# The first mixer's two attentions written as one list of steps

## The chip, the core and the metric

The kernel runs on one core of a Trainium2 chip. A core has five engines with an instruction queue each: TensorE (PE, matrix products; its weight loads are shown apart as PEld), VectorE (DVE), ScalarE (ACT), GpSimd (POOL) and SyncE (SP, which here only issues DMAs). They work on a shared on-chip memory, and PE writes its sums to eight banks of 128 x 512 floats that DVE and ACT read. The metric is the device time of one execution in microseconds, lower is better.

## What is computed

A decoder trunk of two layers on 512 tokens of width 1024, all in float32. Layer 0 has a mixer of two attentions side by side, layer 1 another mixer; each layer ends in a gated ConvFFN. Only the first mixer matters here:

```python
def even_mixer(h, w_in, ...):
    c_q, c_kv, k_rope, dq, dk, dv = split_cols(h @ w_in, EVEN_SPLITS)
    q = heads_first(rms_norm(c_q, cq_g) @ w_uq, MLA_HEADS)        # 8 heads
    kv = heads_first(rms_norm(c_kv, ckv_g) @ w_ukv, MLA_HEADS)
    o_mla = mla_attention(q_nope, q_rope, k_nope, rope(k_rope, pos), v_mla)
    lam = (jnp.exp(jnp.sum(lam_q1 * lam_k1)) - jnp.exp(jnp.sum(lam_q2 * lam_k2)) + lam_init)
    o_diff = diff_attention(dq[:, :, 0], dq[:, :, 1], dk[:, :, 0], dk[:, :, 1], dv, lam, slopes)  # 4 heads
    o_diff = rms_norm(o_diff, subln_g) * (1.0 - lam_init)
    return jnp.concatenate([heads_last(o_mla), heads_last(o_diff)], axis=-1) @ w_out
```

Latent attention is a causal softmax over 8 heads. Differential attention has 4 heads; each takes two softmaxes with a distance bias, and the second, times `lam`, is subtracted from the first before the values are applied.

## The kernel before

The 512 tokens are four tiles of 128 (`NT`), taken in the order 3, 2, 1, 0 (`ORDER`). Products with weights are done in three passes that together keep float32 precision (`mm3`, lines 261 to 265): high part by high part, high by low, low by high. One `mm3` is called a triple here. A weight arrives as a raw tile by a DMA on SP and is split by `Weights.split`: ACT writes the high part (line 72), DVE subtracts it to get the low part (line 73). `Weights.next` hands out the next weight and first splits as many ahead as `depth` says; `load` only issues the DMA. Activations are split alike by `split` (lines 171 and 172).

The instructions are traced in the order of the program, but a planner then chooses the order on each engine from costs that it expects. Only inside `tc.manual_schedule(engines=...)` do the instructions of the engines named stay in the order written. Before the change the mixer has one such block, the output projection at its end.

The mixer (`even`, line 573) has these stages:

- Norm and transposes of x, the compressed projections, and the query/key projections of differential head 0 (lines 618 to 674), then the queries, keys and values of the latent heads (675 to 699).
- Latent attention (701 to 773). A unit is a head pair `p2`, a query tile `i` and a head of the pair `z`: 32 units. `score` (705) makes one score product (line 709), adds the mask and takes the row minimum on DVE (the table-add, line 593), takes the exponential and its sum on ACT (597), and on DVE the reciprocal (712) and the scale (713). `turn` (719) transposes the blocks on PE (727) and copies them out, on ACT for odd heads (737) and on DVE for even ones (739). `value` (742) multiplies by the values once per head pair (750) and splits the result into `oM` (752). `skewed` issues stage d of unit n - d in each round; the value projection of the differential heads, `diff_v` (757), is issued between and after, one tile of 24 matmuls at a time. The planner mixes all of this.
- Differential attention (776 to 905). A unit is a head and a tile: 16 units. `score` makes two score products in two banks (827), two table-adds, two exponentials, and combines them on DVE (838 to 841); `turn` transposes and copies (604 to 609); `value` multiplies (852), scales, squares on ACT (856) and takes the reciprocal root on POOL (178 to 181); `norm` scales again (863); `finish` transposes a whole head and splits it into `oD` (870, 871). Between every second pair of rounds there is a filler: a query/key projection `diff_qk`, and at the end the first half of the output projection's terms for tiles 3 and 2 (`early`). The tables (bias `alibi`, norm gain, `lam`) are loaded at the start of this stage (779 to 797).
- The output projection (910 to 931), a manual block: for each tile two halves of the columns and two halves of the terms (`project`), the residual with its norm, and the next norm's transposes, one tile behind.

Memory tiles come from pools; tiles of one tag share `bufs` buffers, and a tile waits until the one before it in its buffer has been read. Weights' halves have 5 buffers (`wpool`), raw tiles 3, and the eight banks are shared by tags: "a" 3, "s" 2, "t", "n" and "o" 1 each.

Of the kernel before, what the change touches and what calls it, by code (L numbers as in the profile page):

```python
# [9 lines left out]
F32 = mybir.dt.float32  # L10
# [7 lines left out]
P = 128  # L18
S = 512
# [67 lines left out]
def trunk(tc, A, out):  # L87
# [3 lines left out]
    with ExitStack() as top:  # L91
# [5 lines left out]
        GAP = 32  # L97
# [475 lines left out]
        def even():  # L573
            with ExitStack() as es:
# [12 lines left out]
                xh, xl = xnT  # L587

                def softmax_negated(sc, ps, table, n, bufs, reads=None):

                    s = sc.tile([P, S], F32, tag="s", name="s", bufs=bufs)
                    st = sc.tile([P, 2], F32, tag="st", name="st", bufs=6)
                    m = DVE.tensor_tensor_reduce(out=s[:, :n], in0=ps, in1=table, scale=1.0, scalar=3e38,
                                                 op0=ALU.add, op1=ALU.min, accum_out=st[:, 0:1])
                    if reads is not None:
                        reads.append(m.ins.name)
                    ACT.activation(s[:, :n], s[:, :n], AF.Exp, bias=st[:, 0:1], scale=-1.0,
                                   accum_out=st[:, 1:2])
                    return s, st

                def transposed(sc, s, nb, on_act, tag, bufs=3):
                    tp = bank(tag, "tpp", 4, P)
                    for j in range(nb):
                        PE.transpose(tp[:, j], s[:, j * P:(j + 1) * P], ident[:])
                    pt = sc.tile([P, 4, P], F32, tag="pt", name="pt", bufs=bufs)
                    if on_act:
                        ACT.copy(pt[:, :nb], tp[:, :nb])
                    else:
                        DVE.tensor_copy(pt[:, :nb], tp[:, :nb])
                    return pt  # L610


                with ExitStack() as e1:
# [8 lines left out]
                    def diff_qk(h, z):  # L622
                        acc = bank("a", "aqk")
                        wh, wl = W.next()
                        for k in range(KD):
                            mm3(acc, wh[:, k * P:(k + 1) * P], wl[:, k * P:(k + 1) * P],
                                xh[:, k], xl[:, k], k == 0, k == KD - 1)
                        if z == 0:
                            ACT.activation(dq[h], acc, AF.Copy, scale=-0.125)
                        else:  # L630
                            DVE.tensor_copy(dk[h], acc)

                    with ExitStack() as e2:
# [4 lines left out]
                        cT = (cp.tile([P, 3, S], F32R, tag="cth", name="cth"),  # L638
                              cp.tile([P, 3, S], F32R, tag="ctl", name="ctl"))
# [33 lines left out]
                        for z in range(2):  # L673
                            diff_qk(0, z)
# [27 lines left out]
                    mmask = sc.tile([P, S], F32, tag="mmask", name="mmask")  # L702
                    nc.scalar.dma_start(mmask[:], A["mla_mask"])

                    def score(p2, i, z):
                        def f(_):
                            h, w = 2 * p2 + z, (i + 1) * P
                            s_ps = bank("s", "sps")
                            PE.matmul(s_ps[:, :w], mq[h][:, i * P:(i + 1) * P], mk[h][:, :w], start=True, stop=True)
                            s, st = softmax_negated(sc, s_ps[:, :w], mmask[:, 384 - i * P:], w, 3)  # L710
                            rd = sc.tile([P, 1], F32, tag="rd", name="rd", bufs=4)
                            DVE.reciprocal(rd[:], st[:, 1:2])
                            DVE.tensor_scalar(s[:, :w], s[:, :w], rd[:, 0:1], None, ALU.mult)
                            return s
                        return f

                    pts = {}
                    off = (0, 512, 896, 1152, 1280)

                    def turn(p2, i, z):  # L720
                        def f(s):
                            if i == 0:
                                pts[p2, z] = sc.tile([P, 1280], F32, tag="pt", name="pt", bufs=3)
                            pt = pts[p2, z]
                            tp = bank("tn"[z], "tpp", 4, P)
                            for j in range(i + 1):
                                PE.transpose(tp[:, j], s[:, j * P:(j + 1) * P], ident[:])

                            for j in range(0, i + 1, 2):
                                n = min(2, i + 1 - j)  # L730
                                c = off[j] + (i - j) * P
                                d = off[j + 1] - off[j] - P
                                o = pt[:, c:c + P] if n == 1 else pt[:, c:c + 2 * d].rearrange(
                                    "p (a b) -> p a b", a=2)[:, :, 0:P]
                                t = tp[:, j] if n == 1 else tp[:, j:j + 2]
                                if z:
                                    ACT.copy(o, t)
                                else:
                                    DVE.tensor_copy(o, t)
                        return f  # L740

                    def value(p2, i, z):
                        def f(_):
                            if i < NT - 1 or z == 0:
                                return
                            o = bank("o", "o")
                            for j in range(NT):
                                for y in range(2):
                                    h = 2 * p2 + y
                                    PE.matmul(o[y * 64:(y + 1) * 64, j * P:], mv[:, j, h * 64:(h + 1) * 64],  # L750
                                              pts[p2, y][:, off[j]:off[j + 1]], start=(j == 0), stop=(j == NT - 1))
                            split(oM[0][:, p2], oM[1][:, p2], o)
                        return f

                    wv = []

                    def diff_v(i):
                        if not wv:
                            wv.extend(W.next() for _ in range(4))
                        t = slice(i * P, (i + 1) * P)  # L760
                        a = bank("a", "av")
                        for k in range(KD):
                            wh, wl = wv[k // 2]
                            c = slice((k % 2) * 512, (k % 2 + 1) * 512)
                            mm3(a, xh[:, k, t], xl[:, k, t], wh[:, c], wl[:, c], k == 0, k == KD - 1)
                        if i % 2 == 0:
                            DVE.tensor_copy(dv[:, i], a)
                        else:
                            ACT.copy(dv[:, i], a)

                    skewed([[g(p2, i, z) for g in (score, turn, value)]
                            for p2 in range(4) for i in range(NT) for z in range(2)],
                           [lambda i=i: diff_v(i) for i in range(NT)], 100)


                sc = es.enter_context(tc.tile_pool(name="esd", bufs=1, reuse_waits="tile"))
                oD = (sc.tile([P, 4, S], F32R, tag="odh", name="odh"),
                      sc.tile([P, 4, S], F32R, tag="odl", name="odl"))
                subg = sc.tile([P, P], F32, tag="subg", name="subg")
                nc.scalar.dma_start(subg[:], A["ev_subln_g"][0:1, :].partition_broadcast(P))  # L780
                lamb = sc.tile([P, 4, 64], F32, tag="lamb", name="lamb")
                nc.scalar.dma_start(lamb[:], A["ev_lam"].partition_broadcast(P))
                reads = []
                neglam = sc.tile([P, 1], F32, tag="neglam", name="neglam")
                alibi = sc.tile([P, 4, S], F32, tag="alibi", name="alibi")
                nc.scalar.dma_start(alibi[:], A["alibi"])
                lj = sc.tile([P, 64], F32, tag="lj", name="lj")
                ls = sc.tile([P, 2], F32, tag="ls", name="ls")
                for z in range(2):
                    DVE.tensor_tensor_reduce(out=lj[:], in0=lamb[:, 2 * z], in1=lamb[:, 2 * z + 1], scale=1.0,  # L790
                                             scalar=0.0, op0=ALU.mult, op1=ALU.add, accum_out=ls[:, z:z + 1])
# [53 lines left out]
                def turn(h, i):  # L845
                    return lambda s: transposed(sc, s, i + 1, i % 2, "t")
# [552 lines left out]
```

## Time and profile before

| | us |
|---|---|
| runs: median of 3 (lowest, highest) | 1167.63 (1166.95, 1168.72) |
| profiled execution, its span | 1165.2 |
| PE busy | 1145.4 |
| DVE busy | 812.3 |
| ACT busy | 556.9 |
| mean granted clock of PE | 0.998 |

The span of the profiled execution runs from its first to its last instruction. The profile's page has the whole, and the trace behind it answers by line, by stretch of time and by instruction. A row of a group names the line, engine and operation, what it writes and reads, the shapes and the count, then the busy time and the mean length in ns, then how long the engine stood idle just before these instructions and what ended that. In a row of the timeline the first two numbers are the start and the length in us; a bracket at the end has the idle time before it and its releaser.

### The profile page before, as it was taken

What the parts mean: (1) busy time and instruction counts of PE and PEld (TensorE: products, weight loads), DVE (VectorE), ACT (ScalarE), POOL (GpSimd) and SP (SyncE); (2) the same over time, 40 slices, a digit from 0 to 9 for tenths busy, and PEclk for the clock granted to TensorE, in tenths of its full rate; (3) what the DMA queues carried; (4) which work ended last, traced back from release to release, by engine and by line L of the source; (5) the groups of instructions that cost most, each with busy time, mean ns of one, the idle gap of its engine ahead of it and who ended that gap; (6) DMA issues with size and microseconds to landing.
All of it is one profiled execution on the core that took longest, in us unless ns stands there. A gap on an engine that the chain in (4) does not pass through costs nothing.

```text
span 1165.2 us, 15209 instructions
## 1 busy us (share of the span) xinstructions
PE 1145.4 (98%) x5668; PEld 939.9 (81%) x5668; DVE 812.3 (70%) x1431; ACT 556.9 (48%) x940; POOL 57.5 (5%) x137
## 2 busy tenths in 40 slices
PE   8999999999999999999999999999999999999997
PEld 8876667898888888888878877898988888888886
DVE  6677676457766767899873465666676766779896
ACT  5565555245444444456553454544444444445562
POOL 2100012110000000000020000002000000000002
PEclk9999999999999999999999999999999999999999
DMA  8320521033332332354735212322232323324461
GB/s 283 115 64 1 169 73 38 37 130 127 95 104 91 104 95 82 109 159 155 246 108 159 73 55 91 91 74 83 95 116 91 102 98 91 106 84 136 138 214 72
DMA packets 39049, 126.81 MB, mean 109 GB/s; under 512 B 4672, under 2 KB 6336, under 8 KB 38848
## 3 DMA queue, kind: packets, MB, share of 16 engines
q1 hardware_dynamic: 37056, 122.11, 32.8%
q10 hardware_dynamic: 1920, 3.74, 1.0%
q8 instruction: 44, 0.72, 0.3%
q14 instruction: 29, 0.24, 0.1%
HBM read 117.95 MB, written 6.29 MB: 107 GB/s over the span
## 4 chain that ended last, share of the span: by engine, by line
PE 45%; issue 2%; DVE 1%; POOL 1%; ACT 1%; POOLq 0%; DVEq 0%; ACTq 0%
PE u L265 7%; PE u L264 7%; PE u L263 7%; PE acc L263 3%; PE acc L265 3%; PE acc L264 3%; PE apt L263 3%; PE apt L264 3%; PE apt L265 2%; PE cp L1064 1%; PE apv L263 1%; PE apv L265 1%; PE apv L264 1%; PE o L1148 1%; PE o L1225 1%
## 5 line engine op out<-in xcount | busy, mean ns | idle before, releaser
L73 DVE TENSOR_TENSOR wl<-wraw,wh 128x1024 fp32r<-128x1024 f32 (+1 forms) x202 | 244.5, 1218 | 182.2 <-ACT wh L72 178.0
L72 ACT CAST wh<-wraw 128x1024 fp32r<-128x1024 f32 (+1 forms) x202 | 209.4, 1046 | 281.2 <-PE u L264 179.6
L264 PE MATMUL u<-xl,wh 128*128 128x512 f32 (+1 forms) x768 | 285.3, 372 | 0.1
L265 PE MATMUL u<-xh,wl 128*128 128x512 f32 (+1 forms) x768 | 285.2, 372 | 0.0
L263 PE MATMUL u<-xh,wh 128*128 128x512 f32 (+1 forms) x768 | 285.0, 372 | 0.1
L264 PEld LDWEIGHTS u<-xl,wh 128*128 128x128 f32 x768 | 144.7, 188 | 25.3 <-DVE xl L172 0.3
L263 PEld LDWEIGHTS u<-xh,wh 128*128 128x128 f32 x768 | 144.5, 188 | 25.4 <-ACT xh L171 0.6
L265 PEld LDWEIGHTS u<-xh,wl 128*128 128x128 f32 x768 | 144.7, 188 | 24.9
L264 PE MATMUL acc<-wl,gh 128*128 128x512 f32 (+1 forms) x250 | 96.9, 387 | 0.0
L265 PE MATMUL acc<-wh,gl 128*128 128x512 f32 (+1 forms) x250 | 96.9, 387 | 0.0
L263 PE MATMUL acc<-wh,gh 128*128 128x512 f32 (+1 forms) x250 | 96.8, 388 | 0.0
L417 ACT ACTIVATE y<-y 128x512 f32<-128x512 f32 x44 | 27.7, 632 | 85.1 <-DVE y L415 85.1
L412 ACT ACTIVATE y<-u,cw 128x512 f32<-128x512 f32 x88 | 67.4, 773 | 1.8 <-PE u L265 1.8
L415 DVE SCALAR_TENSOR_TENSOR y<-u,cw,y 128x510 f32<-128x510 f32 x88 | 65.6, 748 | 2.5
L413 DVE SCALAR_TENSOR_TENSOR y<-u,cw,y 128x511 f32<-128x511 f32 x88 | 65.1, 744 | 0.9 <-ACT y L412 0.9
L178 POOL TENSOR_TENSOR rv<-ms,epst 128x1 f32<-128x1 f32 x39 | 11.0, 285 | 924.1 <-ACT junk L230 843.9
L263 PEld LDWEIGHTS acc<-wh,gh 128*128 128x128 f32 x250 | 46.9, 188 | 10.0 <-issue 0.6
L265 PEld LDWEIGHTS acc<-wh,gl 128*128 128x128 f32 x250 | 46.9, 188 | 9.7
L264 PEld LDWEIGHTS acc<-wl,gh 128*128 128x128 f32 x250 | 46.9, 188 | 9.6
L263 PE MATMUL apt<-xh,wh 128*128 128x512 f32 x128 | 50.6, 395 | 0.0
L264 PE MATMUL apt<-xl,wh 128*128 128x512 f32 x128 | 50.0, 391 | 0.0
L265 PE MATMUL apt<-xh,wl 128*128 128x512 f32 x128 | 49.9, 390 | 0.0
(305 smaller groups left out, 1911.3 us busy)
## 6 DMA issues: line engine op xcount, KB each, us to landing
wraw<-in_ffn_w_up SPq DMA_DIRECT2D x88, 512.0 KB, 3.6
wraw<-in_ffn_w_down SPq DMA_DIRECT2D x44, 512.0 KB, 3.7
wraw<-in_od_w_dqk SPq DMA_DIRECT2D x12, 512.0 KB, 3.6
wraw<-in_ffn_w_down SPq DMA_DIRECT2D x22, 256.0 KB, 2.6
wraw<-in_ev_w_dqk SPq DMA_DIRECT2D x8, 512.0 KB, 4.0
wraw<-in_ev_w_out SPq DMA_DIRECT2D x8, 512.0 KB, 3.7
spill<-X SPq DMA_DIRECT2D x8, 512.0 KB, 2.6
X<-spill SPq DMA_DIRECT2D x8, 512.0 KB, 6.6
```

Of the source, the lines that this page charges most:

```text
L72: self.nc.scalar.copy(h[:, :w], raw[:, :w])
L73: self.nc.vector.tensor_tensor(l[:, :w], raw[:, :w], h[:, :w].bitcast(F32), ALU.subtract)
L263: PE.matmul(o, lh, rh, start=first, stop=False, skip_group_check=more)
L264: PE.matmul(o, lh, rl, start=False, stop=False, skip_group_check=more)
L265: PE.matmul(o, ll, rh, start=False, stop=last, skip_group_check=more)
L412: ACT.activation(y[:, z], u, AF.Identity, bias=c[:, 3:4], scale=c[:, 2:3])
L413: DVE.scalar_tensor_tensor(y[:, z, 1:], u[:, :S - 1], c[:, 1:2], y[:, z, 1:], ALU.mult, ALU.add)
L415: DVE.scalar_tensor_tensor(y[:, z, 2:], u[:, :S - 2], c[:, 0:1], y[:, z, 2:], ALU.mult, ALU.add)
L417: ACT.activation(y[:, 0], y[:, 0], AF.Silu)
L1064: PE.matmul(zp[:, c + (j2 - j) * P:c + n], tri[:, 0 if j2 == j else 1], part[:, off[j2]:off[j2 + 1]], start=(j2 == j and part is sh), stop ...
L1148: PE.matmul(o12[hp][:, y, r], pt[:, y, rr, g], cv12[:, r, c:c + 64], start=(g == 0), stop=(g == 1))
L1225: PE.matmul(o[:, h], pt[:, h, b * P:(b + 1) * P], cv[:, j0 + b, h * 64:(h + 1) * 64], start=(b == 0), stop=(b == nb - 1))
```

## The change

Latent and differential attention are written out as two loops, one after the other, in manual blocks that name PE, DVE, ACT and POOL. `skewed`, `transposed` and the nested stage functions go. The core of the first loop, with `M` = 32 units:

```diff
+ W.depth = 1
+ wv = [W.next() for _ in range(4)]
+ made = {2: 14, 21: 15, 25: 16, 29: 17}
+ fill = Fill(diff_v((3, 2)), diff_v((1, 0)), *[diff_qk(h, z) for h in range(1, 4) for z in range(2)])
+ with tc.manual_schedule(engines=everything):
+     for n in range(M + 2):
+         if n + 2 in made:
+             W.load()
+         m = n - M
+         if 0 <= n - 1 < M:
+             m_scale(n - 1)
+         if m == 1:
+             d_combine(0)
+         if 0 <= n - 2 < M:
+             m_turn(n - 2)
+         if n < M:
+             m_score(n)
+         else:
+             d_score(m)
+         if n % 8 == 2 and n > 8:
+             o = m_values(n // 8 - 1)
+         fill(1 if n < M else 3)
+         if n % 8 == 3 and n > 8:
+             split(oM[0][:, n // 8 - 1], oM[1][:, n // 8 - 1], o)
+         if n in made:
+             W.ahead(made[n])
+     o = m_values(3)
```

`m_score` is the score product, the table-add and the exponential; `m_scale` the reciprocal and the scale; `m_turn` and `m_values` are the old `turn` and the matmuls of `value`. `Fill` holds generators and issues one triple per count. `diff_v` now takes two tiles at a time, into two "a" banks, with the two tiles' triples of one weight block behind each other:

```diff
+ def diff_v(tiles):
+     accs = [bank("a", "av") for _ in tiles]
+     for k in range(KD):
+         wh, wl = wv[k // 2]
+         c = slice((k % 2) * 512, (k % 2 + 1) * 512)
+         for a, i in zip(accs, tiles):
+             if k or i != tiles[0]:
+                 yield
+             t = slice(i * P, (i + 1) * P)
+             mm3(a, xh[:, k, t], xl[:, k, t], wh[:, c], wl[:, c], k == 0, k == KD - 1)
```

The core of the second loop, with `N` = 16 units; `quota` gives the triples of each step, and `made` the ten steps that end in a weight split (each one's DMA is issued a step earlier):

```diff
+ early = [(i, half) for i in (3, 2, 1) for half in range(2)]
+ fill.parts += [project(*e, 0) for e in early]
+ made = {3: (W, 18), 5: (W, 19), 6: (W2, 1), 7: (W, 20), 8: (W2, 2), 9: (W, 21), 10: (W2, 3),
+         11: (W, 22), 13: (W, 23), 15: (W, 24)}
+ quota = [0, 0] + [5] * 2 + [4] * 8 + [3] * 4 + [4] * 3
+ with tc.manual_schedule(engines=everything):
+     W.ahead(17)
+     split(oM[0][:, 3], oM[1][:, 3], o)
+     for m in range(2, N + 3):
+         if m + 1 in made:
+             made[m + 1][0].load()
+         if 0 <= m - 3 < N:
+             d_norm(m - 3)
+         if m - 1 < N:
+             d_combine(m - 1)
+         if m - 2 < N:
+             d_turn(m - 2)
+         if m < N:
+             d_score(m)
+         n = quota[m]
+         fill(n - n // 2)
+         if m - 2 < N:
+             d_value(m - 2)
+         if (m - 3) % 4 == 3 and m > 3 and m < N + 2:
+             d_finish((m - 3) // 4)
+         fill(n // 2)
+         if m in made:
+             w, k = made[m]
+             w.ahead(k)
...
+     fill.end()
+     d_finish(3)
```

`d_score` is two score products, two table-adds and two exponentials; `d_combine` the four DVE operations that combine them; `d_turn`, `d_value`, `d_norm` and `d_finish` are the old stages (`d_finish` uses bank "n" for heads 0 to 2). The output projection's block follows in the same manual block; tile 1's first half of the terms is now among the early ones.

The rest: a function `tables`, called before the latent heads' queries are made, issues five DMAs on ACT's queue for the bias (in two buffers that the norm used), the mask (into `dv[:, 0]`, which the value projection overwrites only at its end), the norm gain and the lambda vectors, and computes `lam` there; the old loads of these go. The compressed vectors `cT` are now views of `oM`. Score tiles come from a pool `sx` with 4 buffers for both attentions (before 3 and 5). `new_xnT` is called later, `W.depth` is 5 again after the block, and some spacers that place buffers change size.

More of the change, by code (lines that the diff above doesn't have):

```diff
@@ L742, in value @@
[L742 to L769, printed above, removed]
@@ L782, in even @@
[L782 to L791, printed above, removed]
```

322 lines of the change are left out of this document (170 added, 152 removed).

## The prediction

> **What bounds the kernel now.** I read the page's totals first, then the busy time by stage, then the two attention stages in order of time.
>
> ```profile
> span 1165.2 us, 15209 instructions
> PE 1145.4 (98%) x5668; PEld 939.9 (81%) x5668; DVE 812.3 (70%) x1431; ACT 556.9 (48%) x940; POOL 57.5 (5%) x137
> ...
> 64.00:130.80 66.80, 66.70 (x317) 44.55 (x316) 46.65 (x173) 35.91 (x104) 0.00 (x0) 1.00 0.17 53
> 130.80:207.50 76.70, 72.74 (x381) 52.18 (x381) 54.97 (x183) 40.79 (x118) 13.88 (x32) 1.00 0.27 85
> 207.50:242.00 34.50, 34.50 (x163) 28.75 (x162) 15.74 (x21) 13.03 (x28) 5.09 (x16) 1.00 0.11 46
> ```
>
> A stage row reads: length, then busy time of PE, weight loads, DVE, ACT, POOL, then the granted clock. The stages are latent attention with the value projection (64.0 to 130.8), differential attention with the query/key projections (to 207.5), and the output projection (to 242.0, where the first ConvFFN's matmuls begin). PE looks full, but its ends are modelled, so I price its work from start to start.
>
> ```profile
> 65.01 0.39 PE L263 MATMUL av<-wh,xh 128*128 128x512 f32 x1
> 65.69 0.39 PE L263 MATMUL av<-wh,xh 128*128 128x512 f32 x1
> ...
> 84.91 1.88 PE L709 MATMUL sps<-mk,mq 128*128 128x512 f32 x4
> 86.62 0.49 PE L727 MATMUL tpp<-ident,s 128*128 128x128 f32 x3
> 86.95 0.39 PE L709 MATMUL sps<-mk,mq 128*128 128x128 f32 x2
> ...
> 117.46 2.42 PE L750 MATMUL o<-pt,mv 128*64 128x512 f32 x15
> ...
> 132.01 0.92 PE L827 MATMUL sps<-dqk 64*128 64x384 f32 x4 [0.78 <-DVE st L593]
> 140.05 1.16 PE L852 MATMUL o<-dv,pt 128*128 128x128 f32 x8
> ```
>
> Three projection matmuls (one "triple") take 0.68 (65.01 to 65.69). A 512-wide score takes 0.86 (two in 1.71), so 0.215 per block of 128; a transpose 0.11; a head pair's latent values 2.4. A differential score pair costs 0.215 per block too (0.92 less a tail of 0.28, over 3), differential values 0.22 per block. Work in 64.0 to 207.5: 80 latent score blocks 17.2, 80 transposes 8.8, 32 triples 21.8, values 9.6; then 64 triples 43.5, 40 score blocks 8.6, 40 transposes 4.4, 40 value blocks 8.8, 16 closing transposes 1.8. Together 124.5 of 143.5 us: PE loses about 19 us to waits. That is all that a better order can win.
>
> **What the change does, part by part.** It adds no arithmetic. It fixes the order on PE, DVE, ACT and POOL, moves tables and 8 triples of projection (tile 1, first half of the terms) forward, and pairs value tiles.
>
> Is a written list kept literally? The old kernel has one, in the output projection:
>
> ```profile
> 227.99 0.55 POOL L181 TENSOR_TENSOR rr<-rv,mhalf 128x1 f32<-128x1 f32 x1
> ...
> 231.27 0.69 DVE L225 TENSOR_TENSOR t<-ao,gain 128x512 f32<-128x512 f32 x1 [3.84 <-ACT junk L230]
> 231.88 1.40 DVE L876 SCALAR_TENSOR_TENSOR t<-X,rr,gain 128x512 f32<-128x512 f32 x2
> ```
>
> L876 had its scale at 228.54, and DVE idled 3.84, yet it ran after L225, as written. So I take the list as literal.
>
> *Latent list.* Step n puts on DVE: reciprocal and scale of unit n-1, copy of unit n-2 (even heads), table-add with minimum of unit n. The reciprocal of n is then next on DVE, and needs ACT's exponential of n. Nothing stands between, so DVE waits out each exponential, and PE's transposes two steps on wait for that scale.
>
> ```profile
> 67.61 0.28 DVE L593 CUSTOM_DVE_ANT_0 s<-sps,mmask 128x128 f32<-128x128 f32 x1
> ...
> 72.16 0.16 DVE L712 RECIPROCAL rd<-st 128x1 f32<-128x1 f32 x1
> 72.36 0.42 DVE L713 TENSOR_SCALAR s<-s,rd 128x384 f32<-128x384 f32 x1
> ...
> 73.63 0.69 DVE L593 CUSTOM_DVE_ANT_0 s<-sps,mmask 128x512 f32<-128x512 f32 x1
> 74.42 0.72 ACT L597 ACTIVATE s<-s,st 128x512 f32<-128x512 f32 x1
> 75.27 0.16 DVE L712 RECIPROCAL rd<-st 128x1 f32<-128x1 f32 x1
> 75.94 0.48 DVE L713 TENSOR_SCALAR s<-s,rd 128x512 f32<-128x512 f32 x1
> 76.34 0.28 DVE L593 CUSTOM_DVE_ANT_0 s<-sps,mmask 128x128 f32<-128x128 f32 x1
> ...
> L597 ACT ACTIVATE s<-s,st 128x128 f32<-128x128 f32 (+3 forms) x32 | 17.9, 563 | 9.3 <-DVE st L593 7.2 <-DVE rd L712 2.0
> L593 DVE CUSTOM_DVE_ANT_0 s<-sps,mmask 128x128 f32<-128x128 f32 (+3 forms) x32 | 15.3, 482 | 5.0 <-PE sps L709 4.0 <-PE tpp L727 1.0
> L713 DVE TENSOR_SCALAR s<-s,rd 128x128 f32<-128x128 f32 (+3 forms) x32 | 12.3, 383 | 0.6
> L739 DVE COPY pt<-tpp 128x256 f32<-128x256 f32 (+1 forms) x24 | 8.6, 371 | 2.1 <-PE tpp L727 2.0
> L73 DVE TENSOR_TENSOR wl<-wraw,wh 128x1024 fp32r<-128x1024 f32 x3 | 3.6, 1220 | 0.8 <-ACT wh L72 0.8
> L171 ACT CAST omh<-o 128x512 fp32r<-128x512 f32 x4 | 2.3, 586 | 7.2 <-PE o L750 7.2
> L72 ACT CAST wh<-wraw 128x1024 fp32r<-128x1024 f32 x2 | 2.1, 1052 | 0.0
> L172 DVE TENSOR_TENSOR oml<-o,omh 128x512 fp32r<-128x512 f32 x3 | 2.1, 685 | 0.0
> ```
>
> At 512 wide: table-add to exponential 0.79 (0.10 over its length), exponential to reciprocal 0.85 (0.13 over), reciprocal to scale 0.20, scale to the next table-add 0.40 (0.08 under). With the means over the four widths: 0.48 + 0.10 + 0.56 + 0.13 + 0.20 + 0.30 = 1.78 us a unit, 56.9 for 32. Copies: 24 x 0.29 = 7.0. Four weight splits and three output splits stand at the ends of steps, exactly there: ACT's half queues behind the exponential, DVE's half then stands ahead of the next reciprocal. A weight split adds 1.05 + 1.22 less 0.09 of overlap, 2.2, an output split 1.2: 8.8 + 3.6. Sum 76.3 on DVE, against 55.0 of PE work in the same steps (17.2 + 8.8 + 21.8 and three values at 2.4). The old order needed 66.8 for latent attention and the same value triples, as it put other units' DVE work under each exponential.
>
> The first table-add stood at 67.61, right behind a weight split; I keep that start (bounds 65 to 68), so the list's last scale ends at 67.6 + 76.3 = 143.9. Then the last transposes 0.44, a score 0.64, three triples 2.04 and the last values 2.4 bring PE to 149.4.
>
> *Differential list, 17 steps.* Ten steps end in a weight split.
>
> ```profile
> L840 DVE SCALAR_TENSOR_TENSOR s<-s,den 128x512 f32<-128x512 f32 (+3 forms) x16 | 8.8, 550 | 0.0
> L863 DVE SCALAR_TENSOR_TENSOR otok<-otok,rr,subg 128x128 f32<-128x128 f32 x16 | 5.6, 349 | 10.6 <-POOL rr L181 10.5
> L839 DVE SCALAR_TENSOR_TENSOR den<-den,st,neglam 128x1 f32<-128x1 f32 x16 | 3.5, 217 | 1.5 <-ACT s L597 1.3
> L609 DVE COPY pt<-tpp 128x384 f32<-128x384 f32 (+1 forms) x8 | 3.3, 417 | 0.0
> L856 ACT ACTIVATE jk<-otok 128x128 bf16<-128x128 f32 x16 | 4.9, 307 | 12.4 <-DVE otok L854 12.3
> ```
>
> There the loop runs: table-add 0.58 with its hop, two exponentials 1.12, square 0.31, cast 1.05, DVE's half 1.22, then norm 0.27, reciprocals 0.30, the factor 0.22, combine 0.47, and half the time a copy 0.34: 5.7 with mean widths; these ten steps are narrower (2.1 blocks against 2.5) and two of the pieces overlap their neighbours, so 5.35. Ten make 53.5; two head splits among them add 1.0, five evacuations of query/key sums 2.8: 57.3. The seven plain steps run at PE's pace (step 2: four transposes 0.44, a two-block score 0.43, four value blocks 0.88, five triples 3.4): 5.2 + 4.2 + 3.6 + 4.2 + 3.4 + 3.1 + 3.2 = 26.9. Where the two kinds meet, in five places, PE's value matmuls wait for a copy that stands behind the step before's split; I take 1 us each (bounds 0 and 2): 5. The list then ends at 149.4 + 57.3 + 26.9 + 5 = 238.6.
>
> *Output projection.* 34.5 less the 8 moved triples (5.4) is 29.1; the first transposes of the next norm come 0.7 too early for their rows (estimate from 0.69 + 1.40 of DVE after the last sum against 2.7 of PE). End: 268.4 instead of 242.0.
>
> *Costed at nothing.* The pairing keeps its 96 matmuls. The tables: the old mask's issue cost ACT 0.39; five such are 2 us, under an ACT that idles 2.57 twice in that stretch.
>
> ```profile
> 51.15 0.58 ACT L693 COPY mk<-auk 64x512 f32<-64x512 f32 x1 [2.57 <-PE auk L265]
> ...
> 64.07 0.39 ACTq L703 DMA_DIRECT2D mmask<-in_mla_mask  x1
> ```
>
> Without that cover it is 2 us. The old table loads at 120 lay under value triples, so nothing is won there. Loads on SP are issued one to three steps (over 5 us) ahead of their splits.
>
> The sum: +26.4 on 1165.2 is a span of 1191.6; the runs' median lies 2.4 above the span, so 1194.
>
> **The rivals.**
>
> *PE sets the pace after all, and the list removes its waits (faster).* Then the latent list is PE's 55.0, the two first differential steps and the last values 8.0, and the differential steps are 66 triples 44.9, 33 score blocks 7.1, transposes, values and closings 15.0: from 64.0 to 194.0, projection to 223.1, so -19: 1149. For it: the page's 98% on PE. Against: at w = 512 PE has 1.97 a unit, while DVE's and ACT's own chain is 2.24 before copies. It decides only if DVE work can slip under an exponential. The Trainium skill ("Perfetto Trace Analysis", section "Identifying the Most-Contended Engine") says to work on the engine with the highest occupancy; by that rule the filling of PE's gaps is the whole result, which is this rival.
>
> *Only the latent half loses.* The differential waits vanish into PE's work: 149.4 + 67.0 = 216.4, projection to 246.2: +4.2, 1172. For it: there, exponentials have half a step of PE work and the square before DVE needs them. Against: ten splits are queued in DVE's way.
>
> *The list isn't literal* and the planner's order mostly stays: 1168.
>
> A clock loss would top the forecast up. Twice (steps 6 and 10) a head's split and a weight's stand behind each other on DVE, and PE's value matmuls could then wait up to 0.69 + 1.22 + 0.27 + 0.30 + 0.22 + 0.47 + 0.34 = 3.5 us.
>
> ```profile
> 0.00:20.00 20.00, 16.15 (x81) 14.62 (x82) 10.07 (x15) 11.15 (x18) 4.04 (x16) 0.91 0.79 273
> ```
>
> Only where PE idled early was the clock 0.91; the stage rows above have 1.00, and I add nothing. The Trainium skill ("TensorE: Matmul & The Clock Gate", section "Part 1: The HAM clock gate (the "warmup" mystery)") has the clock halve after an idle window of about 3.4 us and stay so for another; by that rule two such waits would cost up to 3.4 us more.
>
> **How the numbers follow.** Forecast 0.74, only the latent half 0.12, PE's pace 0.09, list not literal 0.05. The forecast's own range is 1184 to 1206: 0.10 more or less per hop is 3 us, the seams 5, the start 3, an uncounted wait in each differential step some 5. Reaching down past the second rival gives 1169 to 1206, with about 0.2 outside (the first and third rival, and the forecast's top). A measurement tells 0.2% (2.3 us) from no change. Slower: 0.74 + 0.12 + 0.01 = 0.87; faster 0.09 + 0.02 = 0.11; same 0.02.
>
> **What would show it.** In the latent stage DVE idles before each reciprocal, released by the exponential, about 0.8 a unit, and PE's transposes wait for the scale; the last 32nd unit's scale lies near 144. In the differential stage DVE's half of a split waits 1 to 2.5 us for ACT, and PE's value matmuls wait for DVE's copy. The first ConvFFN matmul lies near 268. I am wrong if reciprocals follow without a wait, or if the first ConvFFN matmul lies before 242.

## The result, and the profile after

The changed kernel takes 1195.81 us (median of 4 runs, 1193.37 to 1197.56) against 1167.43 us for the kernel before on the same chip: a ratio of 1.0241, 95% interval 1.0226 to 1.0255. It is slower by 28.4 us; forecast were 1194 and a range of 1169 to 1206.

The page's head and the busy time by stage for the changed kernel. The first stage ends with the last latent values (in the kernel before, it ended with the rest of the value projection, which came behind them), the second with the start of the last head's closing transposes, the third with the first ConvFFN matmul.

```profile
span 1193.6 us, 15204 instructions
PE 1149.9 (96%) x5668; PEld 939.8 (79%) x5668; DVE 815.0 (68%) x1431; ACT 554.8 (46%) x940; POOL 55.4 (5%) x139
...
64.00:150.80 86.80, 71.52 (x330) 43.92 (x329) 50.19 (x175) 36.81 (x108) 0.46 (x2) 0.96 0.12 37
150.80:239.40 88.60, 77.10 (x388) 56.13 (x387) 53.22 (x173) 37.85 (x113) 11.82 (x32) 0.98 0.20 60
239.40:268.94 29.54, 29.54 (x141) 24.61 (x140) 15.69 (x21) 13.10 (x28) 6.22 (x16) 1.00 0.13 54
```

The instructions are nearly the same in number (15204 and 15209), and over the whole span DVE and ACT are busy for as long as before within 3 us. What grew most is the time in which PE stands still: 15.3 us of the first stage (before 0.1) and 11.5 us of the second (before 4.0). PE's busy time grew too, by 4.8 and 4.4 us: eight triples of the output projection have moved ahead of the third stage, the first holds six triples of the query/key projections instead of three, and the granted clock is below 1.00 in both, which it was not before. The first ConvFFN matmul starts at 268.94 instead of 242.06, 26.9 us later; the rest of the kernel then takes 924.7 us instead of 923.2.

The groups of the latent stage of the changed kernel (64 to 151 us; the last column is the engine's idle time ahead of these instructions, and what ended it):

```profile
L596 ACT ACTIVATE s<-s,st 128x384 f32<-128x384 f32 (+3 forms) x36 | 20.6, 573 | 44.8 <-DVE st L594 44.8
L594 DVE CUSTOM_DVE_ANT_0 s<-sps,dv 128x128 f32<-128x128 f32 (+3 forms) x32 | 15.5, 483 | 3.2 <-PE sps L776 3.1
L793 PE MATMUL tpp<-ident,s 128*128 128x128 f32 x80 | 15.2, 290 | 15.3 <-DVE s L783 15.3
...
L73 DVE TENSOR_TENSOR wl<-wraw,wh 128x1024 fp32r<-128x1024 f32 x6 | 7.3, 1224 | 6.7 <-ACT wh L72 6.7
...
L782 DVE RECIPROCAL st<-st 128x1 f32<-128x1 f32 x32 | 5.2, 162 | 18.3 <-ACT s L596 18.3
```

L594 is the table-add, L596 the exponential, L782 the reciprocal, L783 the scale, L793 the transposes. The reciprocal's group in the kernel before had 3.7 us of idle time ahead of it:

```profile
L712 DVE RECIPROCAL rd<-st 128x1 f32<-128x1 f32 x32 | 5.1, 159 | 3.7 <-ACT s L597 3.4
```

Now DVE waits 18.3 us for exponentials and 6.7 us for casts of weights, and PE then waits 15.3 us for the scale. ACT waits 44.8 us for DVE's table-add. So neither DVE nor ACT is full (50.2 and 36.8 of 86.8 us): each waits for the other in turn. One stretch of the timeline shows two turns of that loop:

```profile
91.55 0.15 DVE L782 RECIPROCAL st<-st 128x1 f32<-128x1 f32 x1
91.74 0.35 DVE L783 TENSOR_SCALAR s<-s,st 128x256 f32<-128x256 f32 x1
92.01 0.42 DVE L804 COPY pt<-tpp 128x256 f32<-128x256 f32 x1
92.24 0.41 PE L793 MATMUL tpp<-ident,s 128*128 128x128 f32 x2 [0.70 <-DVE s L783]
92.34 0.55 DVE L594 CUSTOM_DVE_ANT_0 s<-sps,dv 128x384 f32<-128x384 f32 x1
...
92.99 0.62 ACT L596 ACTIVATE s<-s,st 128x384 f32<-128x384 f32 x1 [2.08 <-DVE st L594]
...
93.73 0.16 DVE L782 RECIPROCAL st<-st 128x1 f32<-128x1 f32 x1 [0.84 <-ACT s L596]
93.93 0.42 DVE L783 TENSOR_SCALAR s<-s,st 128x384 f32<-128x384 f32 x1
94.27 0.55 DVE L594 CUSTOM_DVE_ANT_0 s<-sps,dv 128x384 f32<-128x384 f32 x1
94.50 0.52 PE L793 MATMUL tpp<-ident,s 128*128 128x128 f32 x3 [0.50 <-DVE s L783]
```

From table-add to table-add it is 1.93 us (92.34 to 94.27), of which DVE works 1.1.

In the differential stage (151 to 239.4 us) the same two groups that the forecast named stand out, and the timeline shows one such place:

```profile
L880 PE MATMUL o<-dv,pt 128*128 128x128 f32 x80 | 12.6, 289 | 9.9 <-DVE pt L870 9.8
...
L73 DVE TENSOR_TENSOR wl<-wraw,wh 128x1024 fp32r<-128x1024 f32 x9 | 11.0, 1222 | 10.2 <-ACT wh L72 10.2
```

```profile
178.00 0.69 DVE L172 TENSOR_TENSOR odl<-tpo,odh 128x512 fp32r<-128x512 f32 x1 [1.31 <-ACT odh L171]
...
178.95 1.23 DVE L73 TENSOR_TENSOR wl<-wraw,wh 128x1024 fp32r<-128x1024 f32 x1 [0.26 <-ACT wh L72]
180.09 0.35 DVE L890 SCALAR_TENSOR_TENSOR otok<-otok,rr,small 128x128 f32<-128x128 f32 x1
...
181.28 0.54 DVE L870 COPY pt<-tpp 128x384 f32<-128x384 f32 x1
...
181.87 1.19 PE L880 MATMUL o<-dv,pt 128*128 128x128 f32 x6 [2.57 <-DVE pt L870]
```

A head's split and a weight's split stand behind each other on DVE, then norm, combine and, last, the copy that PE's value matmuls need: PE waits 2.57 us.

### The profile page after: what moved, and what is told of

The parts are those of the page before. It is cut to its first block, busy times and chain, and to the rows that moved or that the text cites. A ratio compares the mean times of both kernels' runs of the same rounds, so it can differ in the third digit from the quotient of the medians.

```text
span 1193.6 us, 15204 instructions
## 1 busy us (share of the span) xinstructions
PE 1149.9 (96%) x5668; PEld 939.8 (79%) x5668; DVE 815.0 (68%) x1431; ACT 554.8 (46%) x940; POOL 55.4 (5%) x139
## 5 line engine op out<-in xcount | busy, mean ns | idle before, releaser
L596 ACT ACTIVATE s<-s,st 128x128 f32<-128x128 f32 (+3 forms) x64 | 35.7, 559 | 83.8 <-DVE st L594 83.8
```

## The experiments

The theory: the list is kept as written, and two places in it make DVE wait for ACT: the reciprocal written right behind its own unit's table-add, and the low half of a split written right behind ACT's cast. The expectations also speak of a layout: the list with the edit, laid out step by step with the durations of the trace. The table has the starts of three instructions in each profile, and the runs' times (two runs each for score first, split halves behind and scale at the step's end, four to ten for the others); all ratios are to the kernel before on the same chip.

| | last latent scale | last closing transposes | first ConvFFN matmul | runs, median | ratio, 95% interval |
|---|---|---|---|---|---|
| before | 115.79 | 207.1 | 242.06 | 1167.4 | |
| changed | 142.60 | 239.4 | 268.94 | 1195.8 | 1.0226 to 1.0255 |
| score first | 129.45 | 225.1 | 254.67 | 1180.6 | 1.0052 to 1.0155 |
| split halves behind | 136.83 | 226.3 | 255.87 | 1181.5 | 1.0062 to 1.0159 |
| both | 128.02 | 216.3 | 245.83 | 1171.7 | 1.0024 to 1.0052 |
| scale at the step's end | 151.27 | 247.9 | 277.42 | 1201.1 | 1.0230 to 1.0327 |
| order left to the planner | 122.91 | 208.9 | 238.49 | 1165.4 | 0.9970 to 0.9989 |
| the same, single value tiles | 124.12 | 209.7 | 239.28 | 1166.3 | 0.9978 to 0.9999 |
| both, copies on ACT | 129.32 | 214.1 | 243.63 | 1169.3 | 1.0004 to 1.0023 |
| the same, turns a step later | 124.61 | 209.4 | 238.92 | 1166.5 | 0.9979 to 0.9997 |
| changed, again | 142.83 | 242.2 | 271.84 | 1196.8 | 1.0237 to 1.0265 |
| changed, waits filled | 142.92 | 238.3 | 267.90 | 1194.0 | 1.0215 to 1.0245 |
| planner, copies on ACT | 123.62 | 207.7 | 237.19 | 1163.9 | 0.9956 to 0.9981 |

Two things limit the comparison of starts. In the kernel before, part of the value projection comes behind the last latent scale, so its first number stands apart. And the first latent table-add starts at 64.5 to 64.6 us in five of the profiles (score first, both, the two of the planner with copies as they were, turns a step later) and at 65.3 to 65.9 in the other seven of the changed versions. The clock goes with it: from 8 to 20 us it is 1.00 in those five and 0.86 in those seven. So differences of up to 1.4 us between profiles can come from there; the times of the runs carry the verdicts.

**Score first.**

```diff
         for n in range(M + 2):
...
+            if n < M:
+                m_score(n)
+            else:
+                d_score(m)
             if 0 <= n - 1 < M:
                 m_scale(n - 1)
...
-            if n < M:
-                m_score(n)
-            else:
-                d_score(m)
```

> The latent list with one edit: in each step the score and table-add of unit n are written ahead of the reciprocal and scale of unit n-1 (in the two steps that cross over, ahead of the first differential combine too). DVE then has a table-add to do while ACT takes the exponential that the reciprocal needs. Theory (DVE waits out each exponential because the reciprocal is written right behind its own table-add): the waits of the reciprocal for ACT, 18.3 us in all, mostly go; by laying out the list step by step with the trace's durations the last latent scale starts near 131 us instead of 142.6 (the layout gives 11.4 less), the differential list after it keeps its length, the first ConvFFN matmul moves from 269 to about 257.5 and the run to about 1184. Rival (the wait is there but PE's work sets the pace in these steps, so the order on DVE does not matter): last scale within 2 us of 142.6, run 1193 to 1197. Second rival (transposes that now stand behind a later scale lose what the table-adds win): last scale at 147 or later, run 1199 or more.

The last scale came at 129.45, 13.2 us earlier (0.9 of it is the earlier start), and the run at 1180.6, some 15 us less and 3 less than expected. Its groups, 64 to 140 us:

```profile
L594 DVE CUSTOM_DVE_ANT_0 s<-sps,dv 128x128 f32<-128x128 f32 (+3 forms) x32 | 15.5, 486 | 10.1 <-PE sps L776 9.7
L793 PE MATMUL tpp<-ident,s 128*128 128x128 f32 x80 | 14.4, 279 | 6.7 <-DVE s L783 6.7
...
L782 DVE RECIPROCAL st<-st 128x1 f32<-128x1 f32 x32 | 5.1, 159 | 0.6 <-ACT s L596 0.4
```

DVE's wait for exponentials fell from 18.3 us to 0.4, PE's for the scale from 15.3 to 6.7. A part of the waiting moved: DVE now waits 9.7 us for PE's score, where it waited 3.1. PE alone did not set the pace in these steps, nor did later scales lose what was won.

**Split halves behind.** `late` and `flush` collect DVE's half of a weight split and issue it behind the next step's table-adds.

```diff
-        self.nc.vector.tensor_tensor(l[:, :w], raw[:, :w], h[:, :w].bitcast(F32), ALU.subtract)
+        low = lambda: self.nc.vector.tensor_tensor(l[:, :w], raw[:, :w], h[:, :w].bitcast(F32), ALU.subtract)
+        if LATE is None:
+            low()
+        else:
+            LATE.append(low)
```

> One edit: DVE's half of each weight split in both lists (the subtraction that makes the low half) is written behind the next step's score and table-adds instead of right behind ACT's cast. Theory (a split at a step's end makes DVE wait for ACT's cast, which is queued behind the exponential, and all that follows on DVE waits with it): the 25 us that DVE now waits for casts mostly become work; by the layout the last latent scale comes 6 us earlier (near 136.5) and the last head's closing transposes 11.5 us earlier (near 228 instead of 239.4), the first ConvFFN matmul near 257.5 and the run about 1184. Rival (ACT, whose exponentials queue behind the same casts, sets the pace of these steps, so that moving DVE's half wins nothing): closing within 3 us of 239.4, run 1193 to 1197.

The last scale came 5.8 us earlier, the closing transposes 13.1 us earlier, the run at 1181.5. In its differential stage (145 to 226.3 us):

```profile
L899 PE MATMUL o<-dv,pt 128*128 128x128 f32 x80 | 12.4, 286 | 4.0 <-DVE pt L889 3.8 <-ACT pt L889 0.2
L86 DVE TENSOR_TENSOR wl<-wraw,wh 128x1024 fp32r<-128x1024 f32 x9 | 11.0, 1219 | 0.0
```

The low halves now wait for nothing (the nine of this group waited 10.2 us in the changed kernel), and PE's wait for the copy fell from 9.8 to 3.8 us. ACT's casts, which were not touched, do not set the pace.

**Both**, the two edits together and nothing else.

> Both edits together: score and table-add ahead of the scale in the latent list, and DVE's half of each weight split behind the next step's table-adds in both lists. Theory: the two waits are different ones and nearly add up; by the layout the last scale lies 13 us earlier (near 129.5), the last closing transposes 19 us earlier (near 220), the first ConvFFN matmul near 250 and the run 1175 to 1178, still above the kernel before. Rival (one of the waits only hides behind the other, so the second edit adds nothing to the first): 1183 to 1185. Rival (with the waits gone PE's pace is reached): 1160 or less.

1171.7 us: 24.1 less than the changed kernel, where the two edits alone won 15.2 and 14.3. That is 24.1 of 29.5: for the most part they add up, as two different waits do. What the two share stays open. The gain was 3 to 6 us above what the layout gave, and PE's pace was not reached.

**Scale at the step's end.** The same place for the reciprocal relative to its own table-add, but behind the transposes.

```diff
-            if 0 <= n - 1 < M:
-                m_scale(n - 1)
-            if m == 1:
-                d_combine(0)
             if 0 <= n - 2 < M:
                 m_turn(n - 2)
             if n < M:
                 m_score(n)
             else:
                 d_score(m)
+            if 0 <= n - 1 < M:
+                m_scale(n - 1)
+            if m == 1:
+                d_combine(0)
```

> One edit in the latent list: the reciprocal and scale of unit n-1 stand at the step's end, behind the transposes of unit n-2 and the score and table-add of unit n. DVE's reciprocal again has a table-add ahead of it, as with the score written first, but PE's transposes of unit n-1 now come only in the next step behind a scale that itself follows the table-add of unit n. Theory (it is the loop over engines that counts, not the place of the reciprocal alone: scale, next step's transposes on PE, score on PE, table-add, scale): by the layout the last scale comes 6 us later (near 148.5) and the run is 1199 to 1202. Rival (hiding the exponential under a table-add is enough, whatever stands around it): like the score written first, last scale near 131 and run near 1184.

1201.1 us, slower than the changed kernel (1200.3 and 1201.9, against 1193.4 to 1197.6). The last scale came 8.7 us later, where the layout gave 6. Its groups, 64 to 152 us:

```profile
L594 DVE CUSTOM_DVE_ANT_0 s<-sps,dv 128x128 f32<-128x128 f32 (+3 forms) x32 | 15.5, 488 | 23.8 <-PE sps L776 23.4
L793 PE MATMUL tpp<-ident,s 128*128 128x128 f32 x77 | 15.4, 298 | 20.6 <-DVE s L783 20.6
...
L782 DVE RECIPROCAL st<-st 128x1 f32<-128x1 f32 x32 | 5.1, 159 | 0.3 <-ACT s L596 0.3
```

The reciprocal's wait is gone here too, and it helped nothing: PE's transposes wait for the scale (20.6 us), its score stands behind them, and DVE's table-add waits for that score (3.1 us in the changed kernel, 23.4 here). The wait moved round the loop. Hiding the exponential is worth something only if no new loop over PE takes its place.

**Order left to the planner.** Everything of the change stays but the literal order of the two attention loops; the output projection behind them keeps a manual block.

```diff
-                    with tc.manual_schedule(engines=everything):
+                    if True:
                         for n in range(M + 2):
...
-                with tc.manual_schedule(engines=everything):
+                if True:
...
                         for m in range(2, N + 3):
```

> The changed kernel with everything kept (early tables, paired value tiles, the value triples spread one to a step, the 8 projection triples moved forward) except that the two attention lists are no longer literal: the planner may choose the order on each engine there, as it did in the kernel before; the output projection stays a literal list. Theory (the loss is the literal order on DVE; tables, pairing and moved triples cost nothing): the run falls back to the neighbourhood of the kernel before, 1160 to 1172. Rival (early tables, paired tiles or the new tile buffers cost the time, whatever the order): 1185 or more.

1165.4 us, 0.2% faster than the kernel before and 30.5 below the changed one. The stages of this run:

```profile
64.00:131.10 67.10, 67.10 (x326) 44.14 (x326) 49.65 (x179) 37.55 (x107) 0.71 (x2) 1.00 0.18 56
131.10:208.90 77.80, 73.72 (x386) 55.05 (x387) 51.33 (x168) 37.53 (x112) 14.48 (x32) 1.00 0.19 62
```

The stage that took 86.8 us takes 67.1, without a gap on PE. So the early tables, the paired tiles, the new buffers and the moved triples, taken together and in the planner's order, do not cost the time; the literal order does.

**Single value tiles**, in that version (the sums of odd tiles are then copied out by ACT, of even ones by DVE):

```diff
-                    fill = Fill(diff_v((3, 2)), diff_v((1, 0)), *[diff_qk(h, z) for h in range(1, 4) for z in range(2)])
+                    fill = Fill(*[diff_v((i,)) for i in ORDER], *[diff_qk(h, z) for h in range(1, 4) for z in range(2)])
```

> The planner's version of the changed kernel, and in it the value projection one tile at a time as before (tile 3, 2, 1, 0) instead of two. Theory (pairing costs nothing and wins nothing: the same 96 matmuls): within 3 us of the planner's version with pairs. Rival (pairing is worth something, since a tile pair uses each weight half twice in a row): 5 us or more above it.

1166.3 us, 1 us more with overlapping intervals: no difference was measured. The pairing in the literal list was not tried.

**Copies on ACT, then turns a step later**, both on top of the version with both edits:

```diff
-                    (ACT.copy if i % 2 else DVE.tensor_copy)(pt[:, :i + 1], tp[:, :i + 1])
+                    ACT.copy(pt[:, :i + 1], tp[:, :i + 1])
```

```diff
-                            if 0 <= n - 2 < M:
-                                m_turn(n - 2)
-                            if n % 8 == 2 and n > 8:
+                            for k in [n - 3] if n < M - 1 else [M - 4, M - 3] if n < M else [n - 2]:
+                                if k >= 0:
+                                    m_turn(k)
+                            if n % 8 == 3 and n > 8:
```

> The version with score first and split halves behind, and in it the differential list's copies of transposed weights on ACT for all row tiles (before: ACT for odd, DVE for even). What still holds up PE there is the value matmuls' wait for DVE's copy, up to 1.7 us, which stands behind a combine that waits for ACT. Theory (seams: a copy written behind DVE's combine and splits makes PE late): by the layout the last closing transposes come 4 us earlier (216.3 to about 212.5) and the run is about 1168. Rival (ACT, with exponentials and casts, is as late as DVE): no change, 1171 to 1173, or slower.

> The version before this one, and in it the latent transposes three steps behind their score instead of two (with one step of catching up at the end). What PE still waits for in the latent list is the scale of the unit whose transposes are next, 0.25 to 0.76 us nine times. Theory (these waits are the lag of the list alone): by the layout the last scale moves from 128.0 to about 125.5 and the run to about 1165, about 0.2% under the kernel before. Rival (with that wait gone ACT's exponential or the copies are the next wait): 1168 or more.

1169.3 and 1166.5 us. The first won 2.4 us in the runs and not 4: the theory holds by direction. From the end of the latent values to the closing transposes it is 3.5 us shorter (77.8 against 81.3), and PE's waits for these copies fell from 4.0 us to 1.4. The second won 2.8 us, and the list, still literal, is then just below the kernel before (0.9988). So this list lost by its order, and not by being written.

**The clock.** The granted clock of 0.96 and 0.98 in two stages was not in the forecast. Seen in windows of 3.41 us, in the changed kernel:

```profile
69.77:73.18 3.41, 1.30 (x6) 1.00 (x7) 2.30 (x7) 1.10 (x4) 0.00 (x0) 1.00 0.25 43
73.18:76.59 3.41, 3.41 (x10) 2.20 (x9) 2.16 (x8) 1.25 (x4) 0.00 (x0) 0.50 0.28 111
114.14:117.55 3.41, 1.49 (x8) 0.86 (x7) 2.31 (x6) 1.03 (x2) 0.00 (x0) 1.00 0.18 14
117.55:120.96 3.41, 3.41 (x9) 1.99 (x8) 1.80 (x6) 1.78 (x5) 0.37 (x1) 0.50 0.38 139
...
179.00:182.41 3.41, 0.84 (x6) 0.54 (x5) 3.16 (x11) 0.35 (x2) 0.00 (x0) 1.00 0.35 73
182.41:185.82 3.41, 3.41 (x12) 2.55 (x10) 0.51 (x2) 1.86 (x7) 0.74 (x2) 0.50 0.20 80
202.89:206.30 3.41, 1.57 (x6) 0.96 (x6) 2.80 (x6) 1.20 (x2) 0.60 (x2) 1.00 0.01 2
206.30:209.71 3.41, 2.55 (x14) 2.00 (x14) 1.76 (x9) 2.13 (x8) 0.69 (x2) 1.00 0.48 154
```

The second number is PE's busy time, the third from the end the clock. Three windows at 0.50 begin 13 and 19 times 3.413 us apart (73.18, 117.55, 182.41), and each follows a window with PE busy for 0.84 to 1.49 us; a window with 1.57 us busy (202.89) was not followed by one. To price this, the changed kernel ran again, and beside it a version that issues throwaway transposes, whose results nobody reads, in the seven longest of PE's waits:

```diff
                         tp = bank("tn"[z], "tpp", 4, P)
+                        for _ in range({2: 14, 21: 12, 29: 12}.get(n, 0)):
+                            PE.transpose(tp[:, 0], ident[:], ident[:])
...
                     o = bank("o", "o", P)
+                    for _ in range({5: 16, 7: 8, 9: 16, 13: 10}.get(m, 0)):
+                        PE.transpose(o[:], ident[:], ident[:])
```

> The changed kernel itself, beside the version with filled waits on the same chip: 1195 to 1196. Its stretches at half clock should again begin a whole number of 3.41 us apart, each right behind such a stretch in which PE was busy for less than 1.55 us of 3.41.

> The changed kernel with its order kept, and throwaway transposes of the identity (0.109 us each; overwritten by the real ones) put on PE into its seven longest waits: 14, 12 and 12 ahead of the latent transposes of units 2, 21 and 29 (waits of 2.36, 1.93 and 1.92 us), 16, 8, 16 and 10 ahead of the values of differential units 5, 7, 9 and 13 (2.57, 1.40, 2.57 and 1.82 us). They end before the wait does, so the order and DVE's chain stay. Theory (the clock halves for 3.41 us behind a window of that length in which PE was busy for less than 0.45 of it, and that costs part of the loss): no stretch at half clock between 60 and 245 us, first ConvFFN matmul 2 to 4 us before 268.9, run 1191 to 1194. Rival (in these stretches DVE sets the pace, so the half clock costs nothing): clock 1.00 too, but the first ConvFFN matmul within 1 us of 268.9 and the run 1195 to 1196. Second rival (the clock follows something else than PE's busy share): half-clock stretches remain in this part.

The windows of the repeat, whose grid lies 1.2 us later in the span, and then those of the version with filled waits:

```profile
115.30:118.71 3.41, 1.47 (x7) 0.92 (x7) 2.85 (x7) 0.39 (x2) 0.00 (x0) 1.00 0.25 60
118.71:122.12 3.41, 3.21 (x12) 2.33 (x11) 1.84 (x7) 1.77 (x6) 0.10 (x1) 0.50 0.24 94
...
204.05:207.46 3.41, 1.25 (x6) 0.68 (x4) 3.08 (x8) 0.87 (x1) 0.35 (x1) 1.00 0.17 12
207.46:210.87 3.41, 3.00 (x10) 2.71 (x11) 1.12 (x6) 1.74 (x7) 0.31 (x2) 0.50 0.36 142
227.94:231.35 3.41, 1.56 (x11) 1.31 (x11) 2.57 (x12) 0.94 (x5) 0.00 (x0) 1.00 0.00 0
231.35:234.76 3.41, 3.41 (x12) 2.83 (x11) 2.04 (x5) 1.54 (x4) 0.74 (x2) 0.50 0.02 5
```

```profile
60.00:150.00 90.00, 76.43 (x380) 49.35 (x380) 52.27 (x177) 40.64 (x113) 0.42 (x2) 1.00 0.12 36
150.00:245.00 95.00, 88.81 (x480) 66.90 (x477) 54.60 (x175) 39.53 (x117) 12.07 (x33) 1.00 0.18 56
```

The repeat took 1196.8 us, a little above the expected range, and its halved windows again followed those with little PE work, one of them with 1.56 us, just above the expected 1.55. With the waits filled the clock is 1.00 from 60 to 245 us.

In the latent list that changed nothing. From the first table-add to the end of the last scale it takes 77.5 us with the waits filled, against 77.7 and 77.4 in the two profiles with two halved windows each: there PE's clock does not set the pace, as the rival said. The differential list did get shorter. From the end of the latent values to the closing transposes it took 87.2 us without a halved window, 88.6 with one (the first profile) and 90.5 with three (the repeat). So each cost some 1.1 to 1.4 us there, if nothing else differs between the profiles. The first ConvFFN matmul came at 267.90, between what the theory and the rival had set against 268.9, and 3.9 us before that of the repeat. The runs went from 1196.8 to 1194.0, with intervals that just overlap. By these figures the clock is worth an estimated 1 to 4 us of the 28, varying with where the windows fall; the runs alone don't prove it.

**Planner and copies on ACT**, the copies' edit above in the version with the order left to the planner.

> The planner's version of the changed kernel, with the differential copies of transposed weights all on ACT. Theory (the copies behind DVE's combine were a seam of the list as of the planner's order): PE's wait of 0.9 us for DVE's copy goes, run about 1163 to 1165. Rival (the planner already places the copies where they do no harm, and ACT becomes late): 1165.4 or more.

1163.9 us, 0.3% faster than the kernel before and the lowest median here. PE's wait of 0.9 us for DVE's copy became one of 0.5 us for ACT's. But the interval overlaps that of the planner's version without this edit, so it is not shown that the copies were a seam in the planner's order too.

## Why the prediction was right

- *The list is literal.* Shown: where the planner may choose, the whole loss of 28.4 us is gone.
- *Latent list.* Forecast was a loop of table-add, exponential, reciprocal and scale on DVE's side, from 67.6 to 143.9. It ran from 65.40 to 143.09, 77.7 us against 76.3. DVE waits 18.3 us for exponentials where 32 times about 0.8 would be 25.6: 0.73 each, in 25 units; in the other seven one of the four weight splits or three output splits stands between, and the wait is counted with it. DVE's waits for the casts there are 6.7 us for weights and 3.6 for outputs. Moving the score takes away the waits for exponentials, moving the low halves those for the casts of weights.
- *The start.* It was kept at 67.6 and came 2.2 us earlier. Before, a weight split and its wait of 0.8 us stood right ahead of the first table-add; this split is written at step 2 now. That term was mis-sized, within its bounds.
- *From the last scale to the last latent values.* 5.5 us were forecast, 7.7 passed. The forecast began with the last transposes, but three triples of the step before still stood ahead of them on PE and held them up until 144.79, 1.7 us after the scale's end:

```profile
142.60 0.49 DVE L783 TENSOR_SCALAR s<-s,st 128x512 f32<-128x512 f32 x1
142.61 0.50 PE L263 MATMUL aqk<-xh,wh 128*128 128x512 f32 x1
...
144.79 0.60 PE L793 MATMUL tpp<-ident,s 128*128 128x128 f32 x4
...
148.43 2.38 PE L811 MATMUL o<-pt,mv 128*64 128x512 f32 x16
```

- *Differential list.* 149.4 to 238.6 was forecast, 89.2 us; it took 88.6. With filled waits, and so without the clock's part, it takes 87.2: the work was sized 2 us too long. The ten splits weren't alike, as the forecast had them: five of the low halves waited 1.5 to 2.3 us for the cast, two 0.26 and three not at all, 10.5 us in all. Ten casts of 1.05 come to the same, so the sum was met and its spread was not. The seams cannot be told from the split steps: PE's waits for DVE's copy add up to 9.8 us, and 5 were set for seams.
- *Output projection.* 29.5 us against 29.8.
- *Costed at nothing.* Tables, moved triples and pairing cost nothing, as a whole (order left to the planner). The clock was set at nothing and is not: this step failed. Two waits of up to 3.5 us were forecast at steps 6 and 10, and the longest is 2.57; by the Trainium skill ("TensorE: Matmul & The Clock Gate", section "Part 1: The HAM clock gate (the "warmup" mystery)") the clock halves after an idle window of about 3.4 us, and the windows run free of the kernel. The free-running windows agree with the trace; that one must be idle does not: PE was busy for up to 1.56 us of 3.41 in windows of these lists that were followed by one at half clock.
- *The rest of the kernel* took 1.5 us more from the first ConvFFN matmul on: one half-clock window at 684 us, in the untouched mixer of layer 1. The 14 matmuls behind its start take 4.68 us from the first start to the last (684.11 to 688.79), and the same 14 take 3.08 in the repeat, at full clock (687.13 to 690.21). So this window cost 1.6 us. The totals of this part alone would not show it: where the clock stays at 1.00 until the last 5 us, they run from 922.6 us (both edits) to 925.7 (planner, copies on ACT), for reasons that stay open. This is in the span of 1193.6 that stands against the forecast 1191.6.
- *Luck in the sum.* The terms missed by -2.2 (start), +1.4 (latent list), +2.2 (to the last latent values), -0.6 (differential list), -0.3 (projection) and +1.5 us (the rest). They nearly cancel, so the total is closer (2.0 us) than its parts were known. The mechanism doesn't hang on that: no miss is over 2.2 us of the 28.4.
- *The rivals.* PE's pace (1149) was not reached by any order tried; the best has 1163.9. That only the latent half loses is excluded by the split halves, of whose 13.1 us more than half came in the differential list.

## What to carry to other kernels

When an order is written by hand, follow each engine's queue by itself: an instruction that needs another engine's answer should have work of another unit ahead of it that covers the answer, and a pair such as cast and subtract counts as such a round trip. Check then whether the edit closes a new loop (scale, transposes, score, table-add): the same wait may only move to another engine. A list repaired in this way came to where the planner's order was, and what else the change brought was worth 0.2% in the planner's order (0.9970 to 0.9989).

## Not expected of the hardware

In these traces PE's clock was granted by windows of 3.41 us that run on through the whole span. In the attention lists of both profiles of the changed kernel, a window with PE busy for at most 1.56 us was followed by one at half clock (8 of 8), and a window with 1.57 us or more was not. Two other profiles with halved windows there agree: score first (one, behind 1.00 us) and scale at the step's end (four, behind 0.86 to 1.35 us; windows with 1.70 and 1.78 were not followed by one). In layer 1 this was not all: the changed kernel's window at 684 us followed one with 2.46 us busy, and so did one at the same place of the program with the split halves behind (671 us) and one with the waits filled (686 us).

```profile
680.75:684.16 3.41, 2.46 (x14) 1.42 (x11) 3.38 (x6) 1.58 (x2) 0.00 (x0) 1.00 0.66 163
684.16:687.57 3.41, 3.41 (x9) 2.73 (x9) 2.50 (x6) 1.61 (x2) 0.00 (x0) 0.50 0.49 144
```

PE's ends are modelled, so its busy time there may not be what the gate sees; what else counts was not tried.
